# A four-layer diffusion backbone: another plan for the layer edges, and adaLN steps moved out of the attentions

## The chip, the cores and the metric

One core of a Trainium2 chip. The metric is the device time of one execution in microseconds (us); lower is better. The kernel before takes 1735.46 us, the median of three runs (1735.09 to 1737.63).

## The reference

The model has four layers of width 1024. 256 latent tokens are carried through all of them; 256 context tokens go along as far as the keys and values of layer 2. Each layer has a token mixer and then a SwiGLU feed-forward (FFN).

```
def modulate(h, shift, scale): return h * (1 + scale) + shift
def adaln(cond, w, b): return jnp.split(silu(cond) @ w + b, 6, axis=-1)
def swiglu(h, w_gu, w_down):
    g, u = jnp.split(h @ w_gu, 2, axis=-1)
    return (silu(g) * u) @ w_down
```

The mixer of layers 0 and 3 is pooling over windows of 2, 4, 8 and 16 tokens, that of layer 1 latent attention (MLA) and that of layer 2 neighbourhood attention (NA). Around each of the eight sub-layers stands the same frame: the tokens are normalized (RMSNorm), scaled and shifted by adaLN, the sub-layer's result is normalized, multiplied with an adaLN gate and added to the tokens. adaLN gives six vectors per layer, from the condition of the latent and of the context tokens.

## The kernel before, in words

**Products.** Every matmul is made of three: a value is split into a high part, rounded, and a low part, the rest, and PE computes high·high, high·low and low·high. Weights come in chunks of 128x1024 (512 KB). SP issues their loads in the order of use into `raw`, a ring of five buffers. ScalarE (ACT) writes the high part `wh` (`prep`, line 161) and VectorE (DVE) the low part `wl` (165), each in five buffers; then the raw buffer is free for the next load.

**adaLN.** The six vectors of four layers are 24 units (l, u). A unit is eight steps, each of which needs one 512 KB load of `in_ada_w`. A step is done in one of two ways (`ada_steps`). On PE it is four products of 32x256 into the PSUM bank `adp` (`products`, line 406). Inside an FFN it is done on DVE, as a multiply and add over 1024 columns (424, 426), once per condition; a unit that ended on DVE needs one more set of products per condition on PE, which picks the sums out of `ff_a`. Then ACT copies the result (451), PE turns it (454) and DVE adds the bias. In an FFN, `w()` does RATE[l] steps each time a new weight chunk is first used. In the attentions the letters `a` of the strings `ORDERS["mo"]` and `["no"]` place a step each, on PE. `finish` ends a unit that was begun, on PE. `need(l, u)` does whatever is still missing of a unit when its values are wanted.

**Layer edges.** Between a sub-layer's last product and the next one's first stands the class `Edge`. Per tile of 128 tokens: ACT squares the result (864), DVE multiplies it with the gate (870, 872), a mean, a root and a reciprocal follow (789, 791, 792), DVE updates the tokens (881), ACT squares these (804), and ACT or DVE scales them into `big` (813, 811). PE turns `big` into PSUM (`make_h`, 916; two slots of the pool `aux`). From a slot ACT or DVE writes the modulated value `t` (935, 937), ACT reads the slot a second time for the high part `rh` (930), and DVE subtracts the two for the low part (940). `head` then runs the first products of the next sub-layer (1087, 1088, 1090). Only at the start, where adaLN's values come late, is the slot read once, into `y` (`late_h`, 951 to 959). The pooling layers add `mix_u` (1008, 1011), `mix_y` (products with a band matrix, 1029) and, at the start, `spread_gate` (1047, copied to SBUF at 1053).

**What sets the order.** The steps of an edge, and the weight splits that fall in its time, are tasks of a planner, `Sched`. Each has engines with a duration in us, tasks to wait for, and a priority. `run` takes the ready task with the lowest priority number, places it at the first free time of an engine, and at the end issues all tasks in the order of their planned starts. An engine then works in that order.

**FFN.** FFN 0 and 1 work on 512 tokens (two streams), with two segments of the hidden width; FFN 2 and 3 on 256, with one. The down product comes in two column halves; its second half is split at `k0`: the part before it runs ahead, the part behind it (`Edge.second`) tile by tile, so that the edge's chain of the first tile can begin.

Of the kernel before, what the change touches and what calls it, by code (L numbers as in the profile page):

```python
# [35 lines left out]
    "mo": "pfSpfSEpDEppfTpfpDpSppfpfEfTSpDfpppVppEppDpTSEpTSDVEfDfffpapfpfpTpSEfTDpSfpppVppfTfEDSEpDTSpVpEfDfTpfSfpSpEpTD"  # L36
        "pfppVEpfTffffDpSaaETSDapEpppDVfTafSoaEaTpSoEoDopVawwwTDToowVawwp",
    "no": "papppSEpfpffpSfffDppESffTpffpfDfffTpfEDpVSfppppfpEpDTfpfppfSTfpffffpEDfSppVETfppDppSppffffppEpppfTfffppfSfDEpV"
        "pppDTSffffpppffffppETpDfSpfpVppETffafDapffpfTSpEppfffppfDfSVTEpfffpfpfDpppfpSTppEfappfDfppfpSoVEoSTSopDwpoETDp"
        "wwoVaEowDaTaaapwTV",  # L40
# [9 lines left out]
RATE = (1.27, 1.27, 0.83, 0.5)  # L50
# [23 lines left out]
class Net:  # L74
    def __init__(self, nc, pools, ins, out, uses=None, order=None):
# [17 lines left out]
        self.order = order  # L93
        self.rec = []
# [110 lines left out]
    def w(self, name, i, n=1):  # L205
# [411 lines left out]
class Slot:  # L617


    def __init__(self, before, old):  # L620
        self.before, self.old = before, old
        self.first, self.users, self.tile = None, [], None


class Sched:
# [9 lines left out]
    def add(self, eng, fn, deps=(), prio=5, order=(), ready=0.0, new=None, slots=(), between=False):  # L635
# [7 lines left out]
        t.new, t.between = new, between  # L643
        self.tasks.append(t)
        return t

    def slot(self, tag, bufs):
        a = self.tags.setdefault(tag, [])
        a.append(Slot(a[-1] if a else None, a[-bufs] if len(a) >= bufs else None))
        return a[-1]  # L650

    def run(self):
# [6 lines left out]
        busy = {e: [] for e in "PDAS"}  # L659
        left = list(enumerate(self.tasks))  # L660

        def place(e, at, dur, between):

            for a, b in busy[e]:
                if between:
                    at = b if a <= at < b - 0.1 else at
                    continue
                if at + dur - self.OVER[e] <= a:
                    break
                at = max(at, b)  # L670
            return at

        while left:
            can = [(t.prio, i, t) for i, t in left if all(d.end is not None for d in t.deps) and all(o.start is not None for o in t.order)]
            assert can, [(t.eng, t.prio) for _, t in left][:5]
            _, i, t = min(can, key=lambda x: x[:2])
# [1282 lines left out]
```

## Time and profile before

| what | value |
|---|---|
| median of three runs | 1735.46 us |
| the profiled execution, its own time | 1739.13 us |
| its span | 1737.4 us |
| mean granted clock of PE | 0.974 of full |
| PE busy | 1635.4 us (94%) |
| DVE busy | 1065.8 us (61%) |
| ACT busy | 754.7 us (43%) |
| bytes moved | 286.66 MB, 165 GB/s over the span |

Durations in this document come from the profiled execution, which is 3.7 us longer than the median. Busy time of PE and of the weight loads (PEld) overlaps. Idle time of an engine counts only where it delays PE's work, which the waits and the chain of waits show.

### The profile page before, as it was taken

The page shows a single profiled execution, that of the slowest core. Times are in us where ns is not written, and L with a number is a line of the kernel's source. Part 1 is how long each engine was busy: PE and PEld are TensorE (multiplying, and loading weights), DVE is VectorE, ACT ScalarE, POOL GpSimd, SP SyncE. Part 2 cuts the span into 40 slices and gives each one's busy share as a digit, 9 for nine tenths or more (in the row PEclk, how much of TensorE's full clock was granted, in tenths as well). Part 3 has the DMA queues.
Part 4 walks back from the last instruction along what each step waited for, and adds up shares of the span by engine and source line. Part 5 has one row for each costly group of instructions (what it writes and reads, how often), then busy time and mean ns, then how long its engine had stood idle before and what let it go on. Part 6 is the DMA issues. An engine that isn't in the chain of part 4 may idle for free.

```text
span 1737.4 us, 24716 instructions
## 1 busy us (share of the span) xinstructions
PE 1635.4 (94%) x9686; PEld 1378.5 (79%) x9686; DVE 1065.8 (61%) x1715; ACT 754.7 (43%) x1348; POOL 34.1 (2%) x42
## 2 busy tenths in 40 slices
PE   5899999999989999899999999999979999769998
PEld 2588888888886777888888888888769997659996
DVE  3567766664657674677545536765657773567554
ACT  4663223222554445522232226654565543464442
POOL 0000000000000110000000000000000000000000
PEclk8999999999999999999999999999989999879999
DMA  8926566554221131365654541433338896228662
GB/s 327 338 68 222 191 194 188 165 171 162 73 85 43 55 122 61 110 205 184 199 193 159 195 157 65 137 113 118 101 127 287 285 303 208 108 95 311 195 186 93
DMA packets 82525, 286.66 MB, mean 165 GB/s; under 512 B 9788, under 2 KB 12648, under 8 KB 82408
## 3 DMA queue, kind: packets, MB, share of 16 engines
q1 hardware_dynamic: 79208, 278.71, 48.2%
q0 software_dynamic: 1760, 5.29, 1.0%
q8 instruction: 76, 1.25, 0.3%
q10 hardware_dynamic: 1440, 1.09, 0.2%
q14 instruction: 41, 0.34, 0.1%
HBM read 283.95 MB, written 1.09 MB: 164 GB/s over the span
## 4 chain that ended last, share of the span: by engine, by line
PE 86%; DVE 6%; ACT 6%; DMA 1%; issue 1%; DVEq 0%; SPq 0%; ACTq 0%
PE acc L354 14%; PE acc L355 14%; PE acc L356 13%; PE acc L362 8%; PE acc L363 8%; PE acc L364 8%; PE adp L406 3%; PE acc L1088 2%; PE acc L1087 2%; PE acc L1090 2%; PE aux L354 1%; PE aux L355 1%; PE aux L356 1%; PE aux L916 1%; DVE wl L165 1%
## 5 line engine op out<-in xcount | busy, mean ns | idle before, releaser
L165 DVE TENSOR_TENSOR wl<-raw,wh 128x1024 fp32r<-128x1024 f32 x321 | 389.1, 1222 | 218.2 <-ACT wh L161 216.7
L161 ACT ACTIVATE wh<-raw 128x1024 fp32r<-128x1024 f32 x321 | 334.3, 1053 | 334.9 <-PE acc L364 159.0
L354 PE MATMUL acc<-rh,wh 128*128 128x512 f32 (+1 forms) x1296 | 439.0, 339 | 0.0
L355 PE MATMUL acc<-rh,wh 128*128 128x512 f32 (+1 forms) x1296 | 436.6, 337 | 0.0
L356 PE MATMUL acc<-rh,wl 128*128 128x512 f32 (+1 forms) x1296 | 436.5, 337 | 0.0
L354 PEld LDWEIGHTS acc<-rh,wh 128*128 128x128 f32 x1296 | 246.0, 190 | 30.5 <-issue 4.1
L356 PEld LDWEIGHTS acc<-rh,wl 128*128 128x128 f32 x1296 | 246.0, 190 | 25.8
L355 PEld LDWEIGHTS acc<-rh,wh 128*128 128x128 f32 x1296 | 246.1, 190 | 25.0
L426 DVE SCALAR_TENSOR_TENSOR ff_a<-raw,sc,ff_a 128x1024 f32<-128x1024 f32 x168 | 209.5, 1280 | 0.2
L362 PE MATMUL acc<-wh,rx 128*128 128x512 f32 x528 | 207.0, 392 | 0.0
L363 PE MATMUL acc<-wl,rx 128*128 128x512 f32 x528 | 205.9, 390 | 0.0
L364 PE MATMUL acc<-wh,rx 128*128 128x512 f32 x528 | 205.7, 390 | 0.0
L391 ACT ACTIVATE rx<-big 128x256 fp32r<-128x256 f32 (+1 forms) x82 | 42.4, 517 | 251.9 <-DVE big L556 251.9
L556 DVE TENSOR_TENSOR big<-big,acc 128x256 f32<-128x256 f32 (+1 forms) x90 | 48.9, 543 | 116.8 <-PE acc L356 96.1
L364 PEld LDWEIGHTS acc<-wh,rx 128*128 128x128 f32 x528 | 99.4, 188 | 20.8
L362 PEld LDWEIGHTS acc<-wh,rx 128*128 128x128 f32 x528 | 99.4, 188 | 20.2
L363 PEld LDWEIGHTS acc<-wl,rx 128*128 128x128 f32 x528 | 99.4, 188 | 20.2
L1087 PE MATMUL acc<-rh,wh 128*128 128x256 f32 x304 | 82.8, 299 | 6.4 <-ACT wh L161 3.2
L1088 PE MATMUL acc<-rh,wl 128*128 128x256 f32 x304 | 81.7, 296 | 6.2 <-DVE wl L165 5.9
L916 PE MATMUL aux<-ident,big 128*128 128x128 f32 x192 | 37.3, 329 | 46.1 <-DVE big L811 27.0
L377 DVE TENSOR_TENSOR rx<-big,rx 128x256 fp32r<-128x256 f32 (+1 forms) x82 | 45.0, 549 | 47.8 <-ACT rx L391 47.8
L916 PEld LDWEIGHTS aux<-ident,big 128*128 128x128 f32 x192 | 25.7, 166 | 58.2 <-DVE big L811 28.7
(239 smaller groups left out, 2267.4 us busy)
## 6 DMA issues: line engine op xcount, KB each, us to landing
raw<-in_ada_w SPq DMA_DIRECT2D x192, 512.0 KB, 4.8
raw<-in_gu SPq DMA_DIRECT2D x176, 512.0 KB, 4.6
raw<-in_dn SPq DMA_DIRECT2D x88, 512.0 KB, 4.3
raw<-in_nwin SPq DMA_DIRECT2D x24, 512.0 KB, 3.7
G<-gate POOLq DMA_DIRECT2D x10, 512.0 KB, 4.8
raw<-in_mwo SPq DMA_DIRECT2D x8, 512.0 KB, 3.5
raw<-in_nwo SPq DMA_DIRECT2D x8, 512.0 KB, 3.9
raw<-in_mwin SPq DMA_DIRECT2D x6, 512.0 KB, 3.4
```

Of the source, the lines that this page charges most:

```text
L161: nc.scalar.activation(out=hi[:, 0:n, :], in_=raw, func=AF.Copy)
L165: nc.vector.tensor_tensor(out=lo[:, 0:n, :], in0=raw, in1=hi[:, 0:n, :].bitcast(F32), op=ALU.subtract)
L354: nc.tensor.matmul(out, wh, ah, start=start, stop=False)
L355: nc.tensor.matmul(out, wh, al, start=False, stop=False)
L356: nc.tensor.matmul(out, wl, ah, start=False, stop=stop)
L362: nc.tensor.matmul(out, ah, wh, start=start, stop=False)
L363: nc.tensor.matmul(out, ah, wl, start=False, stop=False)
L364: nc.tensor.matmul(out, al, wh, start=False, stop=stop)
L426: nc.vector.scalar_tensor_tensor(out=acc[:, i, :], in0=v, scalar=c, in1=acc[:, i, :], op0=ALU.mult, op1=ALU.add)
L916: nc.tensor.transpose(slot.tile[:, o:o + 128], xs.tile[:, j:j + 128], n.ident)
L1087: nc.tensor.matmul(o, wh, hi, start=(k == 0), stop=False)
L1088: nc.tensor.matmul(o, wl, hi, start=False, stop=False)
```

## The change

- The strings of both attentions lose their letters `a` (9 each). RATE goes from 1.27 to 1.3 in FFN 0 and to 1.28 in FFN 1; in FFN 1 the units from (2,2) on are done at RATE_ONE = 2.3 steps per chunk. FFN 2 and 3 call `finish(True)` ahead of their edge. The 24 units are finished earlier: ten steps of unit (1,5) by `finish` in FFN 0, eight of (3,4) by `finish` in FFN 1, and none by `need` in FFN 2.
- `split_h` replaces `late_h` and the two-read path: the slot is read once, into `y`, and both parts are made from `y` in SBUF; the high part may be done by ACT or DVE. In single-stream edges the third pair of transposes goes into `adp`.
- `Sched.run` repeats its placing with randomly changed priorities (SEARCH = 1500) when the kernel is built, and keeps the plan with the earliest end of PE. A plan keeps different engines from reading one PSUM bank at the same time. The multiply with the gate waits for its square, and some durations are changed.
- `mix_y` goes tile by tile outside the start; the gate's copies at the start wait for two earlier results; `k0` in FFN 2 and 3 is 16 instead of 12.

The diff, cut to its core:

```diff
     "bm": "ApAppp444pppApp5AppG4ppppEX5pppNNN55NNvpKpppFpqLppvpnnrpRpppmqmpppp",
-    "mo": "pfSpfSEpDEppfTpfpDpSppfpfEfTSpDfpppVppEppDpTSEpTSDVEfDfffpapfpfpTpSEfTDpSfpppVppfTfEDSEpDTSpVpEfDfTpfSfpSpEpTD"
...
+    "mo": "pfSpfSEpDEppfTpfpDpSppfpfEfTSpDfpppVppEppDpTSEpTSDVEfDfffppfpfpTpSEfTDpSfpppVppfTfEDSEpDTSpVpEfDfTpfSfpSpEpTD"
...
-RATE = (1.27, 1.27, 0.83, 0.5)
+RATE = (1.3, 1.28, 0.83, 0.5)
+
+SEARCH = 1500
+
+RATE_ONE = 2.3
...
-            self.credit += self.rate
+            l, u = self.ada_now[0] if self.ada_now else (self.ada_todo or [(0, 0)])[0]
+            self.credit += RATE_ONE if self.rate == RATE[1] and (l, u) >= (2, 2) else self.rate
...
+        t.banks = [s for s in (new, *slots) if s and s.tag in ("acc", "aux", "adp")]
...
-    def run(self):
+    def run(self, best, search):
...
+        if best is None:
+            rng = random.Random(1)
+            best = [t.prio for t in self.tasks]
+            cost = self.place(best)
+            for r in range(search):
+                width, share = rng.choice((0.05, 0.3, 1.5)), rng.choice((0.01, 0.05, 0.3))
+                some = [p + rng.uniform(-width, width) if rng.random() < share else p for p in best]
+                c = self.place(some)
+                if c <= cost:
+                    best, cost = some, c
+        self.place(best)
+
+        for t in sorted(self.tasks, key=lambda t: (t.start, t.end)):
+            self.emit(t)
+        return best
+
+    def place(self, prios):
...
+            _, i = heapq.heappop(can)
+            n += 1
+            t = tasks[i]
+            deps, order = self.links[i]
+            at = max([t.ready] + [tasks[o].start for o in order])
             options = []
             for e, dur in t.eng.items():
-                s = place(e, max([at] + [d.end + (self.HOP if d.on != e else 0) for d in t.deps]), dur, t.between)
+                s = free(e, max([at] + [tasks[d].end + (self.HOP if tasks[d].on != e else 0) for d in deps]), dur, t.between)
+
+                while e != "P":
+                    hit = [b for x in t.banks for a, b, f in banks[x] if a < s + dur and s < b and f != e]
+                    if not hit:
+                        break
+                    s = free(e, max(hit), dur, t.between)
...
+            bisect.insort(busy[t.on], (t.start, t.end))
+            if t.on != "P":
+                for x in t.banks:
+                    banks[x].append((t.start, t.end + self.HOP, t.on))
+            for j in self.after[i]:
+                left[j] -= 1
+                if not left[j]:
+                    heapq.heappush(can, (prios[j], j))
+        assert n == len(tasks)
+        return busy["P"][-1][1] + 0.02 * sum(t.end for t in tasks) / len(tasks)
...
-            prio = 1 + t // 2 * 1.5
+            prio = 1 + t // 2 * 1.5 - 0.05 * (t % 2)
...
                     def sq(ps=ps, sl=sl, end=end, t=t, col=4 + (h if g is None else g)):
                         k = dict(scale=end) if end is not None else {}
                         nc.scalar.activation(out=n.small("junk", 512, 1)[:, sl], in_=ps()[:, sl], func=AF.Square, accum_out=self.cols(t, col, 1), **k)
-                    sqs.append(s.add({"A": 0.68 if g is None else 0.5}, sq, made, p, slots=(slot,)))
+                    q = s.add({"A": 0.82 if g is None else 0.66}, sq, made, p, slots=(slot,))
+                    sqs.append(q)
...
-                    ys.append(s.add({"D": 0.69 if g is None else 0.42}, gy, made + gdeps, p, slots=(slot,), ready=gready))
-                done[h] = ys[-1]
+                    ys.append(s.add({"D": 0.69 if g is None else 0.42}, gy, [q] + made + gdeps + free, p + 0.02, slots=(slot,), ready=gready))
+                done[h] = ys
...
-                tag = "acc" if late and i == 0 and c == 0 else "aux"
+                tag = "acc" if late and i == 0 and c == 0 else "adp" if len(self.streams) == 1 and dp == 2 else "aux"
...
-                    if late:
-                        self.hs[c, d] = self.late_h(ps, n.Y[4 * c + dp][:, 256 * e:256 * e + 256], a, b, hi, lo, trs, ua, ub, slot, prio)
-                        continue
...
-                    def high(ps=ps, hi=hi, a=a, b=b):
-                        nc.scalar.activation(out=hi, in_=ps(), func=AF.Identity, scale=a, bias=b)
...
-                    def low(tmp=tmp, hi=hi, lo=lo):
-                        nc.vector.tensor_tensor(out=lo, in0=tmp.tile, in1=hi.bitcast(F32), op=ALU.subtract)
-                    w = s.add({"D": 0.5, "A": 0.5}, whole, trs, prio, new=tmp, slots=(slot,))
-                    q = s.add({"A": 0.5}, high, trs, prio, slots=(slot,))
-                    self.hs[c, d] = [s.add({"D": 0.42}, low, [w, q], prio, slots=(tmp,)), q]
-
-    def late_h(self, ps, y, a, b, hi, lo, trs, ua, ub, slot, prio):
+                    self.hs[c, d] = self.split_h(ps, n.Y[4 * c + dp][:, 256 * e:256 * e + 256], a, b, hi, lo, trs, ua, ub, slot, prio)
+                    self.in_y[4 * c + dp] = self.in_y.get(4 * c + dp, []) + self.hs[c, d]
+
+    def split_h(self, ps, y, a, b, hi, lo, trs, ua, ub, slot, prio):
 
         n, s, nc = self.n, self.s, self.n.nc
+        late = ub
 
         def part(on):
             if on == "A":
-                nc.scalar.activation(out=y, in_=ps(), func=AF.Copy, scale=a)
+                if late:
+                    nc.scalar.activation(out=y, in_=ps(), func=AF.Copy, scale=a)
+                else:
+                    nc.scalar.activation(out=y, in_=ps(), func=AF.Identity, scale=a, bias=b)
+            elif late:
+                nc.vector.tensor_scalar(out=y, in0=ps(), scalar1=a, scalar2=None, op0=ALU.mult)
             else:
-                nc.vector.tensor_scalar(out=y, in0=ps(), scalar1=a, scalar2=None, op0=ALU.mult)
-
-        def high():
-            nc.scalar.activation(out=hi, in_=y, func=AF.Identity, bias=b)
+                nc.vector.tensor_scalar(out=y, in0=ps(), scalar1=a, scalar2=b, op0=ALU.mult, op1=ALU.add)
+
+        def high(on):
+            if on == "D":
+                nc.vector.tensor_scalar(out=hi, in0=y, scalar1=b if late else 1.0, scalar2=None, op0=ALU.add if late else ALU.mult)
+            elif late:
+                nc.scalar.activation(out=hi, in_=y, func=AF.Identity, bias=b)
+            else:
+                nc.scalar.activation(out=hi, in_=y, func=AF.Copy)
 
         def low():
-            nc.vector.scalar_tensor_tensor(out=lo, in0=y, scalar=b, in1=hi.bitcast(F32), op0=ALU.add, op1=ALU.subtract)
-        w = s.add({"D": 0.5, "A": 0.5}, part, trs + ua, prio, slots=(slot,))
-        q = s.add({"A": 0.45}, high, [w] + ub, prio)
+            if late:
+                nc.vector.scalar_tensor_tensor(out=lo, in0=y, scalar=b, in1=hi.bitcast(F32), op0=ALU.add, op1=ALU.subtract)
+            else:
+                nc.vector.tensor_tensor(out=lo, in0=y, in1=hi.bitcast(F32), op=ALU.subtract)
+        w = s.add({"D": 0.53, "A": 0.56}, part, trs + ua, prio - 0.06, slots=(slot,))
+        q = s.add({"A": 0.48, "D": 0.32}, high, [w] + ub, prio)
         return [s.add({"D": 0.42}, low, [w, q], prio), q]
...
         if self.end_units:
             self.mix_u(l, 0, 1, "acc", use, done)
             self.mix_y(0, 1, "acc", band, done)
-            self.spread_gate(0, 1, "acc")
+
+            used = [done[0, 0], done[0, 1]]
+            self.spread_gate(0, 1, "acc", used)
             self.mix_u(l, 1, 1.2, "acc", use, done)
-            self.spread_gate(1, 1.2, "aux")
+            self.spread_gate(1, 1.2, "aux", used)
 
             self.behind = lambda: self.mix_y(1, 1.3, "aux", band, done)
         else:
-            self.mix_u(l, 0, 1.2, "acc", use, done)
-            self.mix_y(0, 1.2, "acc", band, done)
+            self.mix_u(l, 0, 0.9, "acc", use, done)
+            self.mix_y(0, 0.9, "acc", band, done)
...
-        for t, h in [(t, h) for h in range(2) for t in tiles] if tag == "acc" else [(t, h) for t in tiles for h in range(2)]:
+        for t, h in [(t, h) for h in range(2) for t in tiles] if self.end_units and c == 0 else [(t, h) for t in tiles for h in range(2)]:
...
-            self.gate[c].append(s.add({"A": 0.58}, copy, [m], prio, slots=(slot,)))
+            self.gate[c].append(s.add({"A": 0.58}, copy, [m] + used, prio, slots=(slot,)))
...
-        k0 = max(0, nk - 2 * W_BUFS)
+
+        k0 = 0 if two else nk - 2 * (W_BUFS - 2)
         begun = [n.acc() for _ in tiles] if k0 else None
         for k in range(k0):
             for t in tiles:
                 product(begun[t], t, 1, k)
+        if not two:
+            n.finish(True)
```

How the order changes, at three places. The first is ACT's order at the edge from the last pooling layer into FFN 3 (`wh<-raw` is the high part of a weight, `junk` a square of the result, `big` the tokens' square or scaled tokens, `rh` the high part of the next input). Before:

```order
L813 ACTIVATE big<-xt,st 128x512
L935 ACTIVATE t<-aux,m_132,mod_135 128x256
L930 ACTIVATE rh<-aux,m_132,mod_135 128x256 x3
L935 ACTIVATE t<-aux,m_132,mod_135 128x256
L930 ACTIVATE rh<-aux,m_132,mod_135 128x256 x2
L935 ACTIVATE t<-aux,m_132,mod_135 128x256
L930 ACTIVATE rh<-aux,m_132,mod_135 128x256 x2
L935 ACTIVATE t<-aux,m_132,mod_135 128x256
L930 ACTIVATE rh<-aux,m_132,mod_135 128x256
L161 ACTIVATE wh<-raw 128x1024 x6
```

and after the change:

```order
L871 ACTIVATE big<-xt,st 128x512 x2
L997 ACTIVATE y_103<-aux,m_132,mod_135 128x256
L997 ACTIVATE y_104<-aux,m_132,mod_135 128x256 x2
L997 ACTIVATE y_105<-adp,m_132,mod_135 128x256
L1009 ACTIVATE rh<-y_105 128x256
L997 ACTIVATE y_105<-adp,m_132,mod_135 128x256
L997 ACTIVATE y_106<-aux,m_132,mod_135 128x256 x2
L1009 ACTIVATE rh<-y_106 128x256
L170 ACTIVATE wh<-raw 128x1024 x2
```

ACT had all eight second reads of the slots (930) and behind them six weight splits in a row; now it has two high parts, made from `y`, and two weight splits behind them. One of the others stands between the last part of the pooling layer's products and the squares of the result:

```order
L1066 ACTIVATE rx_20_146<-acc 128x512
L1066 ACTIVATE rx_18_144<-acc 128x512
L1066 ACTIVATE rx_22_148<-acc 128x512
L170 ACTIVATE wh<-raw 128x1024
L923 ACTIVATE junk,st<-acc,edge 128x256 x6
L849 ACTIVATE st<-st,eps 128x1
```

The second is PE's order. Before, at the end of FFN 2's down product, in the middle of its rows:

```order
L364 MATMUL acc<-wh,rx_27_153 128x512
L406 MATMUL adp<-raw,sc 32x256 x32
L454 MATMUL adp<-ident,ada 128x128 x2
L362 MATMUL acc<-wh,rx_28_154 128x512
L363 MATMUL acc<-wl,rx_28_154 128x512
```

After the change these products are gone from there, and in FFN 0, ahead of its last down segment (`pick` takes sums from DVE), stands:

```order
L364 MATMUL acc<-rh,wh 128x512
L365 MATMUL acc<-rh,wh 128x512
L366 MATMUL acc<-rh,wl 128x512
L416 MATMUL adp<-raw,sc 32x256 x28
L416 MATMUL adp<-ff_a,pick 32x256 x8
L372 MATMUL acc<-wh,rx_16_142 128x512
L373 MATMUL acc<-wl,rx_16_142 128x512
```

28 products are seven steps, and 8 are the two picks of a unit that was begun on DVE; FFN 1 has 20 and 4 in the same place.

The third is PE's order at the edge from FFN 2 into the last pooling layer, with `aux<-ident,big` the transposes. Before:

```order
L362 MATMUL acc<-wh,rh 128x256
L363 MATMUL acc<-wl,rh 128x256
L364 MATMUL acc<-wh,rh 128x256
L916 MATMUL aux<-ident,big 128x128 x4
L362 MATMUL acc<-wh,rh 128x256
L363 MATMUL acc<-wl,rh 128x256
```

and after:

```order
L374 MATMUL acc<-wh,rh 128x512
L976 MATMUL aux<-ident,big 128x128 x4
L976 MATMUL adp<-ident,big 128x128 x2
L976 MATMUL aux<-ident,big 128x128 x4
L976 MATMUL adp<-ident,big 128x128 x2
L976 MATMUL aux<-ident,big 128x128 x4
L372 MATMUL acc<-wh,rh 128x256
```

Before, twelve transposes stood ahead of the pooling layer's products and the last four between them; now all sixteen stand ahead, and four go to `adp`.

## Rows read from the trace of the kernel before

**Rows 1.** The page, part 1: busy time, share, instructions.

```profile
PE 1635.4 (94%) x9686; PEld 1378.5 (79%) x9686; DVE 1065.8 (61%) x1715; ACT 754.7 (43%) x1348; POOL 34.1 (2%) x42
```

**Rows 2.** Waits of PE, whole span: total us, times, longest us.

```profile
PE aux L916 <- DVE big L811: 27.0, 8, 7.5
...
PE aux L916 <- ACT rh L930: 14.4, 13, 2.1
PE acc L1088 <- DVE wl L165: 5.9, 3, 3.7
```

**Rows 3.** Stretches, four edges: us, busy PE PEld DVE ACT POOL, PEclk, DMA, GB/s.

```profile
680.00:714.00 34.00, 27.27 (x170) 24.01 (x170) 23.47 (x57) 25.33 (x55) 0.00 (x0) 0.95 0.18 62
...
1262.00:1300.00 38.00, 27.19 (x136) 22.54 (x135) 22.85 (x44) 26.07 (x50) 0.53 (x1) 0.82 0.29 98
...
1484.00:1521.00 37.00, 26.97 (x150) 23.31 (x149) 20.80 (x46) 18.42 (x42) 0.00 (x0) 0.86 0.15 49
1521.00:1546.00 25.00, 9.75 (x42) 7.86 (x43) 17.68 (x40) 18.64 (x42) 0.00 (x0) 0.59 0.14 42
```

**Rows 4.** Chain of waits, end of FFN 2: start us, us, what.

```profile
1470.08 1.52 PE adp L406 x25
1471.60 7.75 DMA raw<-in_ada_w
...
1481.67 0.43 PE acc L362
```

**Rows 5.** Stretches of 20 us: the start, FFN 1, FFN 2.

```profile
40.00:60.00 20.00, 19.15 (x172) 11.49 (x171) 11.48 (x25) 12.09 (x30) 0.00 (x0) 0.92 0.98 363
840.00:860.00 20.00, 20.00 (x90) 16.57 (x89) 12.32 (x11) 3.75 (x5) 0.00 (x0) 1.00 0.75 241
1320.00:1340.00 20.00, 20.00 (x169) 20.00 (x168) 17.45 (x22) 9.68 (x15) 0.00 (x0) 1.00 0.94 325
```

**Rows 6.** Lines of PE in latent attention: busy us, mean ns, idle before.

```profile
L406 PE MATMUL adp<-raw,sc 128*32 128x256 f32 x64 | 4.7, 388 | 0.0
```

**Rows 7.** Chain of waits, edge into the last pooling layer.

```profile
1497.22 1.23 DVE wl L165
...
1504.49 0.70 PE aux L916 x2
```

**Rows 8.** Waits of PE in 82:110, 440:512 and 1062:1097.

```profile
PE aux L916 <- ACT G L1053: 2.7, 1, 2.7
...
PE aux L916 <- ACT rh L930: 3.5, 3, 2.1
...
PE aux L916 <- ACT rh L930: 2.8, 2, 2.1
```

**Rows 9.** Chain of waits, edge into FFN 2.

```profile
1277.74 0.62 DVE y L870
...
1283.30 0.70 PE aux L916 x2
...
1292.64 0.58 PE acc L1088
```

**Rows 10.** Chain of waits, last pooling layer into FFN 3.

```profile
1516.80 0.88 PE acc L1029 x5
...
1531.34 0.70 PE aux L916 x2
...
1541.30 0.58 PE acc L1088
```

**Rows 11.** Waits of ACT in 1516:1546.

```profile
ACT junk L864 <- DVE y L872: 3.7, 5, 1.7
```

**Rows 12.** Lines of ACT by form, whole span: busy us, mean ns, idle before.

```profile
L930 ACT ACTIVATE rh<-aux,m,mod 128x256 fp32r<-128x256 f32 x72 | 38.7, 564 | 9.5 <-DVE t L937 9.2
...
L391 ACT ACTIVATE rx<-y 128x256 fp32r<-128x256 f32 x7 | 2.7, 406 | 0.0
...
L391 ACT ACTIVATE rh<-aux 128x256 fp32r<-128x256 f32 x4 | 1.5, 370 | 0.0
```

More of the change, by code (lines that the diff above doesn't have):

```diff
@@ L1 @@
+import bisect
 import collections
+import heapq
+import random
 from contextlib import ExitStack
@@ L74, with __init__ @@
 class Net:
-    def __init__(self, nc, pools, ins, out, uses=None, order=None):
+    def __init__(self, nc, pools, ins, out, uses=None, order=None, known=None):
         self.nc = nc
@@ L622, in __init__ @@
         self.first, self.users, self.tile = None, [], None
+        self.busy = []
 class Sched:
@@ L658, in run @@
                     t.order.append(t.new.before.first)
-        busy = {e: [] for e in "PDAS"}
-        left = list(enumerate(self.tasks))
-        def place(e, at, dur, between):
-            for a, b in busy[e]:
+        at = {t: i for i, t in enumerate(self.tasks)}
+        self.links = [([at[d] for d in t.deps], [at[o] for o in t.order]) for t in self.tasks]
+        self.after = [[] for _ in self.tasks]
+        for i, (deps, order) in enumerate(self.links):
+            for d in set(deps + order):
+                self.after[d].append(i)
@@ L665, in place, with free @@
+        for t in sorted(self.tasks, key=lambda t: (t.start, t.end)):
+            self.emit(t)
+        return best
+    def place(self, prios):
+        busy = {e: [] for e in "PDAS"}
+        banks = collections.defaultdict(list)
+        tasks = self.tasks
+        def free(e, at, dur, between):
+            b = busy[e]
+            k = max(bisect.bisect_left(b, (at,)) - 1, 0)
+            for i in range(k, len(b)):
+                x, y = b[i]
                 if between:
-                    at = b if a <= at < b - 0.1 else at
+                    at = y if x <= at < y - 0.1 else at
@@ L667, in place @@
                     continue
-                if at + dur - self.OVER[e] <= a:
+                if at + dur - self.OVER[e] <= x:
                     break
-                at = max(at, b)
+                at = max(at, y)
             return at
[L673 to L676, printed above, removed]
-            at = max([t.ready] + [o.start for o in t.order])
+        left = [len(set(d + o)) for d, o in self.links]
@@ L883, in up @@
                         (nc.scalar if h else nc.sync).dma_start(out=n.out[128 * t:128 * t + 128, 512 * h:512 * h + 512], in_=x)
-                new[h] = s.add({"D": 0.7}, up, [fac, done[h]], prio)
+                new[h] = s.add({"D": 0.7}, up, [fac] + done[h], prio)
             if not close:
@@ L923, in make_h @@
                     ps = lambda slot=slot, e=e: slot.tile[:, 256 * e:256 * e + 256]
-                    if late:
-                        self.hs[c, d] = self.late_h(ps, n.Y[4 * c + dp][:, 256 * e:256 * e + 256], a, b, hi, lo, trs, ua, ub, slot, prio)
-                        continue
-                    tmp = self.slot("t")
-                    def high(ps=ps, hi=hi, a=a, b=b):
-                        nc.scalar.activation(out=hi, in_=ps(), func=AF.Identity, scale=a, bias=b)
-                    def whole(on, ps=ps, tmp=tmp, a=a, b=b):
-                        tmp.tile = n.small("t")
-                        if on == "A":
-                            nc.scalar.activation(out=tmp.tile, in_=ps(), func=AF.Identity, scale=a, bias=b)
-                            return
-                        nc.vector.tensor_scalar(out=tmp.tile, in0=ps(), scalar1=a, scalar2=b, op0=ALU.mult, op1=ALU.add)
@@ L1943, in build @@
             with tc.manual_schedule():
-                net = Net(nc, pools, ins, out, uses, second.rec)
+                net = Net(nc, pools, ins, out, uses, second.rec, second.plans)
                 program(net)
```

31 lines of the change are left out of this document (18 added, 13 removed).

## The prediction

> **What bounds the kernel now.** The page's busy times come first: TensorE (PE) is busy for 94% of the 1737.4 us, the next engine, VectorE (DVE), for 61% [rows 1]. So the time is what PE computes plus the some 100 us in which it has nothing to do, and an edit counts only if it takes matmuls off PE or shortens a wait of PE. Second, PE's waits over the whole span: the largest are the transposes (line 916), which wait 27.0 us for the normalized tile of line 811 and 14.4 us for the PSUM readers of line 930 [rows 2]. Third, a table of stretches places the idle time: subtract PE's busy time from the stretch. The edge from latent attention to FFN 1 loses 34.00 − 27.27 = 6.7 us, the edge into FFN 2 10.8, into the last pooling layer 10.0, into FFN 3 15.3 [rows 3]. Last, the chain of waits, for the places that the change touches.
>
> **1. The adaLN block before the last pooling layer goes.** In the chain of waits PE runs adaLN products at 1470.08, waits 7.75 us for a load of `in_ada_w`, and is back at its own matmuls at 1481.67 [rows 4]. The changed order has no such products there, and nothing is late instead: unit (3,3) is finished an FFN earlier. That is −11.6. The first matmul after the wait took 0.43 us [rows 4], where 90 in 20.00 us, 0.22 each, is full speed [rows 5]; some four such matmuls add −0.9. **−12.5** (bounds −11.6 and −13.5).
>
> **2. The 16 product sets inside the attentions go.** A set is 4 products, two records each; 64 records, 8 sets, took 4.7 us of PE in latent attention [rows 6], and the order has 8 more in neighbourhood attention. Together 9.4, of which some 9.0 would come back if PE never waited behind them. Where the next step waits for a softmax anyway, a set costs nothing, so the gain lies between 0 and −9.0. About half of the sets stand in the ends of the two order strings, where PE runs out of independent work: I take the middle, **−4.5**.
>
> **3. What comes in their place.** Unit (1,5) now ends in FFN 0 and (3,4) in FFN 1, both by `finish`, on PE and in one block ahead of the last down half.
> - FFN 0: 7 raw sets and 2 picks, 9 × 0.5 us (4.7 us for 8 sets is 0.59; 0.5 where they follow one another, my estimate) = 4.5. The 7 loads may be late: the nearest row is the block of part 1, where 8 sets cost a wait of 7.75 us [rows 4]. There the DMA engines were already at 325 GB/s with the loads of FFN 2, in two-stream FFNs at 241 [rows 5]; with more slack the five buffers should be full when the block begins, and two loads of 1.4 us each (524,288 bytes at 363 GB/s) remain to wait for. I take 3.0 (bounds 0 and 7.75): +7.5.
> - FFN 1: 5 raw sets, a pick and two transposes: 3.0, and 1.2 for the hop over ScalarE to the transposes: +4.2. Five loads are what the ring holds, so no wait is taken; the bound is again 7.75.
> - Units (3,1) and (3,3) now end on DVE and need a pick each: +1.1.
> - FFN 1 does more steps on DVE, 2.3 per chunk. A chunk is 24 matmuls, 5.33 us by the 0.22 above. A single-condition step is one instruction over 1024 columns, taken at 1.23 us as the weights' low part of that size [rows 7]; with that low part DVE has 3.3 × 1.23 = 4.1 us per chunk plus the gated units. It lies under the matmuls and costs nothing; if the cover is too thin in loads, that is the last rival.
>
> Sum **+12.8**, and adaLN as a whole −12.5 − 4.5 + 12.8 = **−4.2**.
>
> **4. The layer edges.** The same work stands in another order; PE computes the same matmuls. An edge can gain no more than its idle time, and nothing if the new order is no better.
> - Start to FFN 0: the gate is now spread and copied ahead of the context tiles' transposes, so that the 2.7 us for which PE waited for line 1053 [rows 8] go: −2.5 (0 to −2.7).
> - FFN 0 to latent attention and FFN 1 to neighbourhood attention: PE waits 3.5 and 2.8 us for line 930, the second read of a PSUM slot [rows 8]. With one read the slot comes free an instruction earlier: −2 and −2.
> - Latent attention to FFN 1: idle 6.7 [rows 3], the same kinds of wait; −4.5.
> - Into FFN 2: the second tile's transposes stand at 1283.30, the head's matmuls follow at 1292.64 [rows 9], and waiting for a weight's low part is what holds line 1088 [rows 2]. With the weights split ahead of `h` that wait goes. The multiply with the gate (1277.74, 0.62 us [rows 9]) stood ahead of the square in this chain; it now follows, so the chain is 0.7 shorter: transposes at 1282.6, 3.1 us for them (four groups of 0.70 and one short wait for a slot), head at 1285.7. 1285.7 − 1292.6 = −6.9 (0 to −10.8).
> - Into the last pooling layer: the transposes stand at 1504.49 behind a weight's low part at 1497.22 that DVE did in the middle of the norm [rows 7]. The same chain into FFN 2 is 2.5 shorter without it; with 0.4 for the square and −0.9 because PE no longer leaves the pooling products for four transposes, −3.8 (0 to −10.0).
> - Into FFN 3: the band products start at 1516.80, the last transposes at 1531.34, 14.5 later, and the head at 1541.30 [rows 10]. ScalarE's squares and DVE's multiplies read the same PSUM tiles by turns; ScalarE waited 3.7 us for that [rows 11]. With the multiply behind its square, and different banks at a time, some 3 of it go: transposes at +11.5, 3.1 for them as above, 1531.4, with the weights split before. 1531.4 − 1541.3 = −9.9 (0 to −15.3).
>
> Sum −2.5 − 2 − 2 − 4.5 − 6.9 − 3.8 − 9.9 = **−31.6** (0 to some −52).
>
> **A price that speaks against it.** The high part is now read from SBUF. ScalarE's plain 128x256 copy took 406 ns from SBUF and 370 from PSUM, 36 more; but the read that it replaces has scale and bias and took 564 [rows 12]. The form as a whole is 158 ns cheaper and off PE's path mostly: I put it at nothing. [...]
>
> **The sum.** −4.2 − 31.6 = −35.8 against the profiled execution of 1739.13: 1703.3. That execution is 3.7 above the median of the three runs, 1735.46; against the median, 1735.46 − 35.8 = 1699.7, so **1700.0**.
>
> **Rivals.**
> - *Half of the edges' gain.* The order is the best that a search finds on the planner's constants; where an instruction takes longer on the chip, engines wait in the planned order for what is late. For it: the present order was planned with such constants too and has waits of 7.5 us [rows 2]. Then −4.2 − 15.8 = −20: **1716**.
> - *More.* The attentions give back all 9.0, FFN 0's loads are in time, and the edges give 4.5 more: −4.5 − 3 − 4.5 = −12 more: **1688**.
> - *The change doesn't do what it says.* The planned order gains nothing on the chip, and adaLN only moves, with 4 us more of late loads: −4.2 + 4 = 0, **1735**.
> - *Slower: FFN 1 becomes bound by loads.* From unit (2,2) on, a chunk brings 3.3 loads of 524,288 bytes in 5.33 us: 325 GB/s. In FFN 1 the DMA engines moved 241 GB/s with PE full [rows 5]; were that all they give there, a chunk would last 7.2 us, 1.8 longer, and with 28 such chunks +50: **1750**. It decides as soon as they give under 325. Against it: in FFN 2 325 GB/s flowed with PE full all the same, and 363 at the start [rows 5], so 241 was what was asked. [...]
>
> **How the numbers follow.** Forecast 0.60, half 0.18, more 0.12, no change 0.05, slower 0.05. The range, 1688 to 1717, takes in the first three; late loads of the two blocks at their bounds (+12.5) still lie in it. A measurement of this kernel tells 0.2%, 3.5 us, from no change. Faster by more: 0.60 + 0.18 + 0.12 = 0.90; same 0.05; slower 0.05.
>
> **What would show it.** Right: no wait for `in_ada_w` ahead of the last pooling layer; no adaLN products in the attentions; PE's idle time in the three edges behind neighbourhood attention down from 36 to about 16 us; a head of FFN 3 that waits for transposes and not for `wl`; FFN 1 with PE full at over 300 GB/s. Wrong: PE waiting for `wh` or `raw` in FFN 1; transposes that wait longer for the single PSUM read than for line 930; a block in FFN 0 with over 8 us of waiting for `in_ada_w`.

## The result, and the profile after the change

The changed kernel takes 1692.24 us (median of four runs, 1688.81 to 1693.83), the kernel before 1736.55 in four runs: 44 us faster; the ratio of the means is 0.9739, 95% interval 0.9718 to 0.9761. The forecast was 1700.0, its range 1688 to 1717. The profiled span went from 1737.4 to 1690.0, 47.4 less; that is some 3 us more than the medians give, as the profiled execution of the kernel before is 2.6 us above its median.

The page, part 1 (busy us, share, instructions), answers to [rows 1]:

```profile
PE 1620.8 (96%) x9622; PEld 1371.9 (81%) x9622; DVE 1081.3 (64%) x1767; ACT 728.4 (43%) x1309; POOL 33.5 (2%) x42
```

PE's idle time fell from 102.0 us (1737.4 − 1635.4) to 69.2 (1690.0 − 1620.8), 32.8 of the 47.4. The other 14.6 are busy time. 64 adaLN records fewer are some 4.7 of it [rows 6], and 6.5 of the rest is work that ran at full clock (worked out under 4 below): the mean granted clock rose from 0.974 to 0.984; as the granted clock stands in both traces at 0.50 (before, 648.0 to 650.5 us) or at 1.00 (655 to 680 us), that is 2 × 0.026 × 1737.4 = 90 us at half speed before and 54 now.

PE's largest waits over the whole span (total us, times, longest) answer to [rows 2]:

```profile
PE aux L976 <- DVE big L869: 18.5, 6, 7.2
PE adp L416 <- ACT big L862: 8.8, 1, 8.8
PE adp L416 <- DMA raw<-in_ada_w: 6.9, 8, 2.1
PE adp L464 <- ACT ada L461: 4.6, 7, 1.2
```

The transposes still wait for the normalized tile, 18.5 us instead of 27.0. The waits for a second PSUM reader (14.4) and for a weight's low part (5.9) are no longer among the large ones. The 8.8 us stand ahead of adaLN's first products, in the first microseconds of the run; before, PE waited 9.5 us in that place, and the profile put it down to `in_ada_w`. Line 461 is ScalarE's copy ahead of adaLN's transposes, which was line 451 before:

```profile
PE adp L454 <- ACT ada L451: 3.0, 6, 0.5
```

The four edges of [rows 3], in the table of stretches (us, busy time of PE, PEld, DVE, ACT, POOL, then PEclk, DMA, GB/s), at their new places:

```profile
673.00:707.00 34.00, 34.00 (x250) 32.11 (x249) 24.33 (x62) 23.14 (x51) 0.00 (x0) 1.00 0.25 83
1257.00:1288.00 31.00, 26.35 (x157) 23.74 (x156) 19.80 (x44) 18.74 (x38) 0.00 (x0) 0.89 0.50 162
1462.00:1485.00 23.00, 17.71 (x108) 15.40 (x107) 18.58 (x44) 17.33 (x40) 0.00 (x0) 0.85 0.21 70
1485.00:1510.00 25.00, 17.38 (x130) 16.78 (x130) 16.27 (x44) 15.58 (x39) 0.53 (x1) 0.86 0.30 103
```

The edge into FFN 1 has no idle time left (6.7 before). Into FFN 2, the last pooling layer and FFN 3 it is 4.7, 5.3 and 7.6 us instead of 10.8, 10.0 and 15.3.

For the rest of the document the span is cut into stages. A stage ends where the first products behind an edge (`head` of FFN 0, the attentions' input, and so on) have ended in the trace; the last pooling layer lies in FFN 2's stage. Columns are differences in us to the kernel before, from one profiled execution each; a stage that an experiment does not touch still differs by 1 to 3 us.

| kernel | start | FFN 0 | MLA | FFN 1 | NA | FFN 2, pool | FFN 3 | span |
|---|---|---|---|---|---|---|---|---|
| before, us | 121.8 | 379.2 | 225.2 | 368.8 | 210.8 | 248.9 | 182.8 | 1737.4 |
| forecast | −2.5 | +5.5 | −6.8 | +3.3 | −9.2 | −26.2 | 0 | −35.8 |
| the change | −7.4 | +3.3 | −12.7 | +7.3 | −8.3 | −28.4 | −1.2 | −47.4 |
| adaLN moves alone | +0.6 | +6.0 | −3.5 | +11.1 | −1.3 | −13.6 | −0.8 | −1.5 |
| plan alone | −4.4 | −5.2 | −7.8 | −3.8 | −7.1 | −12.9 | −0.5 | −41.7 |
| no search | −2.2 | +5.2 | −3.3 | +8.4 | −8.6 | −25.8 | −1.2 | −27.6 |
| two reads | −4.8 | +1.5 | −11.1 | +7.3 | −7.6 | −24.0 | −1.2 | −39.9 |
| neither rule | +5.4 | +3.0 | −11.5 | +11.6 | −10.8 | −25.4 | −0.6 | −28.3 |
| all units on DVE | −5.9 | −2.6 | −11.2 | +2.2 | −9.0 | −25.9 | −1.2 | −53.7 |

### The profile page after: what moved, and what is told of

Same layout as the page of the kernel before. It is cut to its first block, busy times and chain, and to the rows that moved or that the text cites. A ratio compares the mean times of both kernels' runs of the same rounds, so it can differ in the third digit from the quotient of the medians.

```text
span 1690.0 us, 24597 instructions
## 1 busy us (share of the span) xinstructions
PE 1620.8 (96%) x9622; PEld 1371.9 (81%) x9622; DVE 1081.3 (64%) x1767; ACT 728.4 (43%) x1309; POOL 33.5 (2%) x42
## 4 chain that ended last, share of the span: by engine, by line
PE 77%; DVE 6%; ACT 3%; issue 1%; DMA 1%; POOL 0%; DVEq 0%; ACTq 0%; POOLq 0%
PE acc L364 12%; PE acc L365 12%; PE acc L366 12%; PE acc L372 8%; PE acc L374 8%; PE acc L373 8%; PE aux L364 1%; PE acc L1146 1%; PE acc L1145 1%; PE acc L1148 1%; PE aux L365 1%; PE aux L366 1%; PE aux L1743 1%; PE adp L416 1%; PE aux L976 1%
## 5 line engine op out<-in xcount | busy, mean ns | idle before, releaser
L364 PEld LDWEIGHTS acc<-rh,wh 128*128 128x128 f32 x1296 | 246.2, 190 | 29.0 <-issue 2.9
L366 PEld LDWEIGHTS acc<-rh,wl 128*128 128x128 f32 x1296 | 246.3, 190 | 25.9
L365 PEld LDWEIGHTS acc<-rh,wh 128*128 128x128 f32 x1296 | 246.3, 190 | 25.0
L436 DVE SCALAR_TENSOR_TENSOR ff_a<-raw,sc,ff_a 128x1024 f32<-128x1024 f32 x177 | 221.0, 1279 | 1.0
L1146 PE MATMUL acc<-rh,wl 128*128 128x256 f32 x304 | 78.1, 286 | 0.0
L1427 ACT ACTIVATE big<-big,mx 128x512 f32<-128x512 f32 (+1 forms) x64 | 42.5, 665 | 60.6 <-DVE big L1582 31.7
L1145 PEld LDWEIGHTS acc<-rh,wh 128*128 128x128 f32 x304 | 59.5, 196 | 0.1
```

What stands on the lines that cost most here:

```text
L364: nc.tensor.matmul(out, wh, ah, start=start, stop=False)
L365: nc.tensor.matmul(out, wh, al, start=False, stop=False)
L366: nc.tensor.matmul(out, wl, ah, start=False, stop=stop)
L436: nc.vector.scalar_tensor_tensor(out=acc[:, i, :], in0=v, scalar=c, in1=acc[:, i, :], op0=ALU.mult, op1=ALU.add)
L1145: nc.tensor.matmul(o, wh, hi, start=(k == 0), stop=False)
L1146: nc.tensor.matmul(o, wl, hi, start=False, stop=False)
```

## The experiments

Each kernel was run beside the kernel before, so two versions are compared by their two ratios. The two intervals together leave some 5 us open: a difference below that is not clear of the noise.

### The two halves of the change

The kernel before with the strings, rates, RATE_ONE and `finish(True)` of the change:

```diff
...
-RATE = (1.27, 1.27, 0.83, 0.5)
+RATE = (1.3, 1.28, 0.83, 0.5)
+
+RATE_ONE = 2.3
...
```

> The kernel before with only the adaLN steps moved: the strings without a, the new rates, RATE_ONE and finish(True); planner, edges and PSUM reads as before. Theory A (the prediction's sum, with the attention sets given back whole, since latent attention lost 12.7 us and not 6.7): -12.5 - 9 + 12.8 = -8.7, so about 9 us faster than the kernel before. Rival B (adaLN's move pays nothing by itself; the whole gain is the plan's): within 3 us of the kernel before.

1737.49 us against 1737.29, ratio 0.9999 (0.9989 to 1.0009): rival B. By stage nothing is missing from the gains (−3.5, −1.3, −13.6); FFN 0 and FFN 1 take it all back, +6.0 and +11.1. PE's groups of adaLN instructions in FFN 1 (busy us, mean ns, idle before) show where; first the kernel before:

```profile
L406 PE MATMUL adp<-ff_a,pick 128*32 128x256 f32 x64 | 4.7, 388 | 0.0
...
L454 PE MATMUL adp<-ident,ada 128*128 128x128 f32 x8 | 1.5, 272 | 0.0
```

and with the moved steps:

```profile
L409 PE MATMUL adp<-ff_a,pick 128*32 128x256 f32 x96 | 7.2, 388 | 1.7 <-DVE ff_a L429 1.7
L457 PE MATMUL adp<-ident,ada 128*128 128x128 f32 x14 | 2.8, 284 | 2.3 <-ACT ada L454 2.3
L409 PE MATMUL adp<-raw,sc 128*32 128x256 f32 x40 | 2.6, 386 | 0.7 <-DMA raw<-in_ada_w 0.7
```

Picks +2.5, transposes +1.3, raw sets (a step's products on PE) +2.6, and waits of 4.7 us where there were none: 11.1.

The other half, the changed kernel with the old strings and rates, no `finish(True)`, and:

```diff
-                tag = "acc" if late and i == 0 and c == 0 else "adp" if len(self.streams) == 1 and dp == 2 else "aux"
+                tag = "acc" if late and i == 0 and c == 0 else "aux"
```

> The changed kernel with the adaLN steps where they were (old strings and rates, no finish(True)), and with all transposes of the edges in aux, as the bank adp is taken by adaLN there. Theory A (the parts add): the rest of the 44 us, about 35 faster than the kernel before. Rival B (the plan pays only if no adaLN block lies in FFN 2): the block of 11.6 us and the edge behind it eat more than their own time, so 25 us faster or less.

1696.46 us, ratio 0.9763 (0.9748 to 0.9777), 41 us faster: theory A, and more than its 35. So the plan alone brings nearly all; its 4 us to the changed kernel are not clear of the noise. The stage of the last pooling layer shows the two halves apart: −13.6 from adaLN's block, −12.9 from the plan, −28.4 together.

### What in the plan does it

```diff
-SEARCH = 1500
+SEARCH = 0
```

> The changed kernel with SEARCH = 0: the new rules and durations of the planner, with the priorities as written. Theory S (the gain of the edges behind neighbourhood attention is the order's, and the order is the search's): half of the edges' gain is lost, 15 to 20 us slower than the changed kernel. Rival R (the single read, the multiply behind the square and the banks kept apart give nearly all): at most 4 us slower than the changed kernel.

1708.93 us, ratio 0.9835 (0.9819 to 0.9851): 16.7 slower than the changed kernel by the two ratios (0.0096 × 1737), as theory S has it in size but not in place. (Its profiled execution is 2.7 us above its median, so the stages show 20.) Behind neighbourhood attention it loses only 2.3 us (−8.6 and −25.8 against −8.3 and −28.4). It is the start (5.2) and the edge into FFN 1 (9.4 in the stage of MLA) that the written priorities do badly. PE's waits of this kernel show the edge's old wait for the multiply with the gate, which the search removed:

```profile
PE aux L976 <- DVE big L869: 27.3, 8, 9.9
...
PE acc L1145 <- DVE y L930: 3.3, 1, 3.3
```

Next the second read of PSUM, put back everywhere but at the start:

```diff
-        q = s.add({"A": 0.48, "D": 0.32}, high, [w] + ub, prio)
+        if late:
+            q = s.add({"A": 0.48, "D": 0.32}, high, [w] + ub, prio)
+        else:
+            def again():
+                nc.scalar.activation(out=hi, in_=ps(), func=AF.Identity, scale=a, bias=b)
+            q = s.add({"A": 0.56}, again, trs, prio, slots=(slot,))
```

> The changed kernel with the high part read by ScalarE from PSUM a second time, as before, and the search run anew for it. Theory A (a slot comes free an instruction earlier with one read, which is what the two-stream edges gained): 6 to 10 us slower than the changed kernel, with PE waiting at the transposes for the second read again. Rival (the search finds an order that hides the second read): within 3 us of the changed kernel.

1697.23 us, ratio 0.9764 (0.9748 to 0.9781): about 4 slower than the changed kernel, between the two expectations and not clear of the noise. The two-stream edges, where PE waited 3.5 and 2.8 us for the second read, lose nothing with it, so with the order searched anew the single read is not what they gained by. What it may cost lies in the stage of FFN 2 and the last pooling layer (−24.0 instead of −28.4) and at the start (−4.8 instead of −7.4). The one large wait for the second read that PE has left is 1.8 us, where they were 14.4:

```profile
PE aux L976 <- ACT rh L1021: 1.8, 1, 1.8
```

Then the two rules on squares, multiplies and PSUM banks, both taken out:

```diff
-                while e != "P":
+                while False:
...
-                    ys.append(s.add({"D": 0.69 if g is None else 0.42}, gy, [q] + made + gdeps + free, p + 0.02, slots=(slot,), ready=gready))
+                    ys.append(s.add({"D": 0.69 if g is None else 0.42}, gy, made + gdeps + free, p + 0.02, slots=(slot,), ready=gready))
```

> The changed kernel without two of the planner's rules: the multiply with the gate need not wait for its square, and different engines may be planned on one PSUM bank at a time. Theory (squares and multiplies on one bank go by turns, 3.7 us of ScalarE's waits in the last edge): 5 to 9 us slower than the changed kernel, most of it at the edges behind neighbourhood attention. Rival (the search avoids such pairs by itself): within 2 us.

1711.22 us, ratio 0.9846 (0.9826 to 0.9865): 19 slower than the changed kernel, far over the expected 5 to 9, and in another place: 12.8 of it at the start. The first 114 us of this kernel, and then of the changed one, in the table of stretches:

```profile
0.00:114.00 114.00, 82.44 (x660) 55.51 (x661) 56.45 (x147) 58.48 (x145) 0.19 (x4) 0.84 0.72 261
```

```profile
0.00:114.00 114.00, 93.60 (x767) 63.22 (x768) 62.52 (x163) 64.09 (x155) 0.19 (x4) 0.91 0.76 269
```

PE did 107 records less there, at a lower clock, and its waits for `in_ada_w` grew from 3.7 to 15.2 us:

```profile
PE adp L416 <- DMA raw<-in_ada_w: 15.2, 8, 3.8
```

A buffer is free for the next load only when its weights are split or its products done, so an order that delays those delays the loads. SP's waits point that way: in these 114 us its longest wait for adaLN's products (line 416) is 6.3 us, in the changed kernel 2.7. That this is the cause was not tested by itself.

The rules one at a time; first only the wait for the square, then only the banks taken out:

> The changed kernel without one of the two rules taken out together before: the multiply with the gate need not wait for its square; banks are still kept apart. Taken out together they cost 19 us, 12.8 of them at the start. Theory (the banks' rule alone keeps squares and multiplies from going by turns; the wait for the square adds nothing): within 3 us of the changed kernel. Rival (the wait for the square is what shortens the chain by 0.7 us at each edge): 3 to 6 us slower, at the edges behind neighbourhood attention.

> The changed kernel with different engines planned on one PSUM bank at a time, the multiply still behind its square. Theory: most of the 19 us, 12 to 19 slower than the changed kernel, with the start the longest. Rival (with the multiply behind its square no pair of engines is left that meets often on a bank): within 4 us.

1698.19 (0.9775, 0.9755 to 0.9795) and 1696.96 (0.9764, 0.9747 to 0.9780): 6 and 4 slower than the changed kernel, the 4 not clear of the noise. Both together cost 19, so with these orders either rule covers for most of the other: theory's 12 to 19 for the banks alone fell, and the 4 are at its rival's limit; "within 3 us" for the square fell too. Without the wait for the square the loss is at the last edges (−24.3 instead of −28.4 in that stage), as its rival had it. The turns that the rules are meant to stop show the same: at the edge into FFN 3 ScalarE waited 3.7 us for DVE's multiplies [rows 11]; the profile lists no such wait in the changed kernel or with the banks free, 0.2 us with the multiply free, and 1.7 without both rules.

The split of the down product:

```diff
-        k0 = 0 if two else nk - 2 * (W_BUFS - 2)
+        k0 = 0 if two else nk - 2 * W_BUFS
```

> The changed kernel with k0 at 12 as before in FFN 2 and 3. Theory (the later split point only changes how much of the down product is done tile by tile, which the chain of the first tile does not need): within 2 us of the changed kernel. Rival (it keeps weights for the chain's time): 3 us slower or more.

1700.04 us, ratio 0.9782 (0.9761 to 0.9803): 7 slower, the rival. The profiled execution is 3.2 us above the median and shows 11.5, of which 6.0 are in the stage of FFN 2 and the last pooling layer (−22.4 instead of −28.4), and the rest in stages that this edit does not touch. In that stage PE now waits for a weight's high part among the pooling layer's products:

```profile
PE acc L372 <- ACT wh L170: 2.5, 1, 2.5
```

Each of these kernels was also searched along another path, so the last test changes the seed alone:

```diff
-            rng = random.Random(1)
+            rng = random.Random(2)
```

> The changed kernel with another seed of the search, nothing else. The runs that took one rule away each came out 4 to 8 us slower, and each of them also searched along another random path. Theory (the rules are worth these 4 to 8 us): within 2 us of the changed kernel, 1692. Rival (another path of the search costs that much by itself, and those single verdicts are not the rules'): 1695 or more, 3 to 8 us slower than the changed kernel.

1690.22 us, ratio 0.9724 (0.9709 to 0.9739), not slower than the changed kernel's 0.9739. So the losses of 4 to 7 us are not what any other path costs. One seed does not show how wide paths scatter, however: by stage this one differs by up to 3 us, and single losses of that size stay unsettled. The 19 us without both rules, too, come from one path of the search.

### A faster version

The experiment with adaLN alone says that FFN 0 and FFN 1 take back the gain, in raw sets, picks and waits. In this version RATE 1.48 in FFN 0 and RATE_ONE 2.2 in FFN 1 let every unit behind the start be summed on DVE:

```diff
-RATE = (1.3, 1.28, 0.83, 0.5)
+RATE = (1.48, 1.28, 0.83, 0.5)
-RATE_ONE = 2.3
+RATE_ONE = 2.2
```

> The changed kernel with RATE 1.48 in FFN 0 and RATE_ONE 2.2 in FFN 1, so that every unit behind the start is summed on DVE and ends with its picks: FFN 0 seven units, FFN 1 nine, FFN 2 three; no raw product sets in finish. Theory (what adaLN gained in the attentions and in FFN 2 was paid back in FFN 0 and FFN 1 as raw sets on PE and waits of the finish blocks: +6.0 and +11.1 us in the run with adaLN alone): 6 to 9 us faster than the changed kernel, about 1684. Rival (FFN 0's DVE is full at 1.48 two-condition steps per chunk, and PE waits for weights there): same or slower than the changed kernel.

1685.09 us, ratio 0.9693 (0.9676 to 0.9710), 8 us faster than the changed kernel by the ratios. FFN 0 gains 5.9 of the stage, FFN 1 5.1. DVE is not full in FFN 0:

```profile
140.00:180.00 40.00, 38.77 (x182) 31.10 (x181) 31.03 (x34) 12.62 (x16) 1.27 (x2) 1.00 0.61 196
```

It is busy for 31.0 of 40 us, and PE lost 1.2 to picks that waited. In FFN 1 the waits for line 461 stay, and none for `ff_a` or a load:

```profile
PE adp L464 <- ACT ada L461: 3.3, 5, 1.2
```

The other way, with the attentions' sets back, lower rates (1.27 in FFN 0, RATE_ONE 1.6) and all transposes in `aux`:

> The changed kernel with the attentions' strings as before (their 16 sets back on PE), RATE 1.27 in FFN 0, RATE_ONE 1.6, and all edge transposes in aux: one unit more than before in FFN 1 on DVE, none by finish as raw sets, no need block in FFN 2. Theory (the need block alone was worth its 12 us, and the sets in the attentions were cheaper there, 3.5 and 1.3 us, than in FFN 0 and FFN 1): 5 to 8 us faster than the changed kernel. Rival (aux for all transposes and the sets in the attentions cost the same as the finish blocks): within 3 us of the changed kernel.

1687.44 us, ratio 0.9706 (0.9687 to 0.9726), 6 faster than the changed kernel, as its theory has it. So it was enough to remove the block in FFN 2; taking the sets out of the attentions was not needed. Last, four times the search on the version before it:

> The version with every unit summed on DVE (RATE 1.48, RATE_ONE 2.2), with SEARCH = 6000. Theory (the search is near what the planner's constants can tell, PE's waits at the last edges are the chain itself): within 2 us of that version with 1500. Rival (more search finds more): 3 us faster or more.

1681.26 us, ratio 0.9675 (0.9658 to 0.9693): the lowest time of all, 3 us below 1500 tries, but the interval overlaps theirs (0.9676 to 0.9710), so that more search pays is not shown.

## Why the prediction was right

The sign, the range and the main cause, the edges, were right. The time was 8 us too high, and the span's change 11.6 too small (some 3 of these are the slower profiled execution before). That it came so near is in part luck: adaLN brought 4 us less than forecast and the edges some 10 more.

**1. The block in FFN 2.** −12.5 forecast, −13.6 measured in the stage with adaLN alone. Right in sum. Two readings in it were not: the 7.75 us in the chain are no idle time of PE, which did further sets meanwhile and waited 4.7 us for the loads; and unit (3,3) is not finished an FFN earlier but on DVE inside FFN 2, which has the picks of two units.

**2. The sets in the attentions.** −4.5 forecast; −3.5 and −1.3, so −4.8, the second within the scatter of a stage. Right, and for the reason given: PE does 8.6 us less in the two stages but is idle 3.7 us more. The last sets in neighbourhood attention covered a wait for softmax, which now shows. PE's waits there, of the changed kernel:

```profile
PE acc L365 <- DVE pt_pt L387: 1.8, 1, 1.8
```

It was 0.4 before.

**3. What came in their place.** +12.8 forecast, +17.1 measured. FFN 0 was near: 7.5 forecast, 6.0 measured, with 1.4 us given back by the clock; the chain of waits of the changed kernel has the block that was put together there:

```profile
406.70 1.04 PE adp L416 x16
407.76 4.61 DMA raw<-in_ada_w
412.37 0.04 issue
412.41 2.67 PE adp L416 x24
415.08 0.43 PE acc L372
```

8.4 us from the first set to the next matmul, of which PE was idle 2.6 (3.0 taken); seven sets were to be 3.5 and two picks 1.0. The term of FFN 1 is the one that was mis-sized: 4.2 and 1.1 against 11.1. Of these 5.3, 4.1 were work (five raw sets, three picks, one pair of transposes) and 1.2 one hop, the author's estimate; measured were 6.4 of work and 4.7 of waits. Ten units end in FFN 1 instead of six, each with picks and mostly with transposes, and three transposes, a pick and a raw set came too early for their copies, sums and loads. PE's waits in FFN 1 of the changed kernel:

```profile
PE adp L464 <- ACT ada L461: 2.3, 3, 1.2
PE adp L416 <- DVE ff_a L436: 1.7, 1, 1.7
PE adp L416 <- DMA raw<-in_ada_w: 0.6, 1, 0.6
```

adaLN as a whole was to bring −4.2 and brought nothing that the runs can tell from zero.

**4. The edges.** −31.6 forecast, 41 measured with the plan alone. By the table, the three edges behind neighbourhood attention were to give 20.6 and gave 20.0 (−7.1 and −12.9). The start and the three edges before it were to give 11.0 and gave 21.2 (−4.4, −5.2, −7.8, −3.8): these four terms were too small. PE's idle time in the four stages fell by 18.0 us, as the prediction took one wait at the start and parts of the waits of the others.

The bound "an edge can gain no more than its idle time" failed too. The stage up to the edge from FFN 0 to latent attention gained 5.2 with 3.5 idle at the edge; 3.4 came from idle time and 1.4 from the clock. Late in or behind many of its waits PE's clock was granted at half speed for a while, before the change for 3.4 us (0.50 from 647.3 to 650.7) to 20.5 us (from 1524.5 to 1545.0), and the work in that time took twice as long, as the first matmul of 0.43 us against 0.22 in part 1 of the prediction. In [rows 3] the edge into FFN 1 stands at 0.95 over 34 us, 3.4 us at half speed, so 1.7 us of work lost on top of 6.7 idle; in the changed kernel, with no wait there, the clock stays at 1.00. (With the plan alone that stage loses as much to half speed as before, in other places.) The prediction priced this at one place only, behind the block of adaLN (−0.9). Half of PE's busy time at half speed, summed over the span, is what the clock cost: 27.6 us before, 24.6 with the plan alone and 21.1 in the changed kernel. So of the 41.7 us that the span lost with the plan alone, 35.1 are idle time, 3.0 the clock's, and 3.7 work of PE that no experiment traced; of the whole change's 47.4, 6.5 are the clock's.

The start gained 7.4 in the changed kernel where 2.5 was forecast from one wait. The prediction looked only at the last 30 us of it. All kernels with the new plan start 2 to 8 us earlier but the one without both rules.

The edge into FFN 3 was forecast in detail. From PE's timeline and from the chain of waits before:

```profile
1528.02 1.12 PE L916 MATMUL aux<-ident,big 128*128 128x128 f32 x4 [7.48 <-DVE big L811]
```

```profile
1532.07 0.57 ACT t L935
```

and the chain after the change:

```profile
1481.38 3.02 PE acc L1087 x21
...
1492.59 1.12 PE aux L976 x4
...
1494.60 0.55 DVE y L1001
...
1496.90 0.16 PE acc L1145
```

From the band products to the head it is 15.5 us (14.6 forecast, 24.5 before [rows 10]). The head follows the transposes at once and does not wait for `wl`. Where it was gained needs care: the 14.5 us that the prediction gives for "the last transposes" are those of the second of four groups. The first group stood at 11.2 us before (1528.02 − 1516.80) and still stands at 11.2 (1492.59 − 1481.38), so the wait for the first normalized tile is as long as it was (7.5 and 7.2 us). The first read of a turned slot came at 15.3 and now comes at 13.2. So 2.1 of the 9.0 us were gained ahead of that read, where 3.0 were forecast, and 6.9 behind it, as forecast.

**5. The price against it and the slow rival.** ScalarE's high part from SBUF took 416 ns, the one from PSUM 564 [rows 12], and DVE did 46 of them in 292:

```profile
L1009 ACT ACTIVATE rh<-y 128x256 fp32r<-128x256 f32 x26 | 10.6, 416 | 2.1 <-DVE y L1001 1.5
...
L1005 DVE TENSOR_SCALAR rh<-y 128x256 fp32r<-128x256 f32 x46 | 13.0, 292 | 2.6 <-ACT y L997 1.9
```

The rival with loads as the bound had its term wrong: a unit that is done on DVE counts as 11 steps, of which only 8 bring a load, so 1 + 2.3 × 8/11 = 2.7 loads per chunk and 263 GB/s, not 325. FFN 1 moved 252 with PE full:

```profile
840.00:880.00 40.00, 40.00 (x188) 31.91 (x187) 21.96 (x21) 10.26 (x13) 0.00 (x0) 1.00 0.74 252
```

So the sign "over 300 GB/s in FFN 1" did not come, and FFN 1 was not bound by loads. The 363 GB/s of the start are no ceiling either; the kernel before moved more over ten microseconds:

```profile
20.00:30.00 10.00, 5.28 (x43) 1.79 (x42) 5.65 (x10) 4.66 (x9) 0.00 (x0) 0.80 1.02 402
```

## What to carry to other kernels

Price a wait of TensorE as its idle time and the half-speed work behind it, here 102.0 and 27.6 us over the span before, the second read from the granted clock of the stretch. When small work is moved under cover, count every instruction that still ends on the bound engine, and whether its inputs are there when the engine reaches it in the planned order (PE waited 4.7 us for such inputs in FFN 1): moving adaLN from the attentions gave back on PE what it saved. An order worked out by search on plain constants was worth 17 us here, and two rules that each seemed to do little were worth 19 together, each figure from one path of the search.

## What was not expected of the hardware

A wait of the same length is not always followed by half speed. In latent attention PE waits 2.1 us for `big` in both kernels, with as much busy time around it. Ten microseconds around that wait, in the kernel before and then in the changed one (columns as above):

```profile
643.00:653.00 10.00, 7.73 (x36) 6.26 (x36) 6.30 (x17) 3.55 (x8) 2.01 (x3) 0.83 0.16 54
```

```profile
1227.00:1237.00 10.00, 8.44 (x36) 6.50 (x35) 7.39 (x23) 5.36 (x14) 0.00 (x0) 0.83 0.04 15
...
637.00:647.00 10.00, 7.75 (x44) 6.30 (x42) 7.04 (x18) 4.46 (x9) 2.67 (x4) 1.00 0.23 73
```

Before, the clock stands at 0.83 there, in the changed kernel at 1.00; and a wait of 1.6 us in neighbourhood attention, the other row, has 0.83. What decides it is left open. A stage can therefore change by the 1.7 us of such a stretch without a change of its code, which is part of the scatter between the kernels above.

The start moved more than expected through the order alone: without the two rules PE was busy for 11 us less of the first 114, with the same loads to wait for. Whether another path of the search would lose as much there is open.
